# Six buffers for left forms and four for raw weights in the up projection of a hybrid block's gated MLP

## The chip, the cores and the metric

The kernel runs on one core of a Trainium2 chip as a single program. The metric is the device time of one execution in microseconds. Three runs of the kernel before gave a median of 2439.43 us (2439.18 to 2440.35).

## The reference

One decoder block on x of 1024 tokens by 1024 channels: three token mixers side by side (HGRN2, differential attention, RWKV-7), gated and projected; a cross attention to 256 memory tokens; a gated MLP with a causal convolution of width 3; a final RMSNorm. All in float32. The change lies in the MLP:

```python
def conv_gated_ffn(h, w_up, conv_w, conv_b, w_down):
    u, v = jnp.split(h @ w_up, 2, axis=-1)          # 1024 -> 2 x 2816
    u = lax.conv_general_dilated(u, conv_w[:, None, :], window_strides=(1,),
                                 padding=[(CONV_W - 1, 0)],
                                 dimension_numbers=('NWC', 'WIO', 'NWC'),
                                 feature_group_count=D_FF) + conv_b
    return (jax.nn.silu(u) * v) @ w_down            # 2816 -> 1024
```

## The kernel before, in words

Every float32 matrix product is made of three products of a shorter type: each operand is split into a high part (a cast) and a low part (the rest), and hi·hi, hi·lo and lo·hi are summed in PSUM.

**Up projection** (`ffn_up`). The 2816 channels of u and of v are worked through in 22 pairs f = 0 to 21, of 128 channels of u and 128 of v. Instead of the eight block products of a 2 x 2 by 2 x 2 block product, seven are made, of sums of blocks (the scheme of Strassen and Winograd). A pair loads two raw weight tiles of 512 KB (`load`, L1345, on the SP queue): the first holds blocks A11 and A12, the second A21 and A22. From them `left` makes up to seven **left forms** in this order: A11, S2, S3, S1, A12, A22, S4, of which S1 to S4 are sums that POOL makes (L1311). Each form becomes a tile `wf`: its high part is cast by ACT (L1318), its low part is subtracted (L1319) by DVE and POOL in turn. `prod` (L1326) multiplies a form with a right form of the activations: 12 matmuls of 128x512, named here after the right form: A11 with B11, S2 with T2, S3 with T3, S1 with T1, A12 with B21, A22 with T4, S4 with B22. So T2(f) is the product of pair f that needs S2, and B22(f), which needs S4, is the last of its pair. For the first six pairs (`ne` = 6) the products B11 and B21 are made ahead (`ahead`), between the transposes of the trunk before, and kept in DRAM; these pairs have 5 products, or 60 matmuls, left, the others 7, or 84.

DVE reads the products: u2 (L1386) after T2, u3 (L1388) after T3, the halves of vt (L1390, L1395) and of u (L1397). Then come the convolution and the gate: y by ACT (L1399), two steps on DVE (L1400, L1401), SiLU on ACT (L1402), the product with vt (L1403) and the store to DRAM (L1404).

**Buffers.** The forms have 4 buffers: the tags whi and wlo of a pool, two each, and a form uses them in turn. The raw tiles of the pairs have 6: two of the tag raw, and the tags r2 to r5 of the pool `res`, one each; the raw tiles of the six pairs ahead have four, raw twice, r4 and r5. r2 and r3 hold the trunk's normalised rows until its last transposes.

**Down projection** (`ffn_down`). The weights of each of 22 steps (wdr, 512 KB, L1445) go into r2, r3, r4, r5 in turn; wd is their cast on ACT (L1449) and their rest (L1450, POOL for even f, DVE for odd f), ap the same for the activations acr (L1447, L1452, L1453); 48 matmuls follow per step (L1439, ps_dn).

**What sets the order.** The program is written pair by pair; the compiler's scheduler then puts the instructions of each engine into an order of its own by a simulated timeline, and hands out the buffers of a tag in that order. So PE takes products of neighbouring pairs in alternation, and an instruction that waits holds up all behind it on its engine or queue.

Of the kernel before, what the change touches and what calls it, by code (L numbers as in the profile page):

```python
# [96 lines left out]
class K:  # L97
# [1197 lines left out]

    def left(self, r1, r2, which, sp):

        nc = self.nc  # L1300
        V, A, G = nc.vector, nc.scalar, nc.gpsimd
        q = {f"A{n}{k + 1}": r[:, 4 * k:4 * k + 4, :] for n, r in ((1, r1), (2, r2)) if r is not None for k in range(2)}
        sums = {"S1": ("A21", "A22", ALU.add), "S2": ("S1", "A11", ALU.subtract), "S3": ("A11", "A21", ALU.subtract),
                "S4": ("A12", "S2", ALU.subtract)}

        def get(n):
            if n not in q:
                a, b, op = sums[n]
                a, b = get(a), get(b)
                q[n] = sp.tile([P, 4, P], F32, tag=n, name=n, bufs=2 if n in ("S1", "S2") else 1)  # L1310
                G.tensor_tensor(out=q[n], in0=a, in1=b, op=op)  # L1311
            return q[n]

        for n in which:
            x = get(n)
            self.nform = getattr(self, "nform", 0) + 1
            f = self.wp.tile([P, 2, 4, P], F32R, tag=("whi", "wlo")[self.nform % 2], name="wf")
            A.copy(out=f[:, 0], in_=x)  # L1318
            (V if self.nform % 2 else G).tensor_tensor(out=f[:, 1], in0=x, in1=f[:, 0].bitcast(F32), op=ALU.subtract)  # L1319
            yield f  # L1320
# [9 lines left out]
    def ffn_up(self, X, act, part, spill):  # L1330

        nc, tc, I = self.nc, self.tc, self.I
        V, A, G, T = nc.vector, nc.scalar, nc.gpsimd, nc.tensor
        with tc.tile_pool(name="up", bufs=1) as sp:
            col = lambda j, f: self.pc("ffn_conv_w", NFF * j + f) if j < 3 else self.pc("ffn_conv_b", f)
            nraw = itertools.count()
            u = sp.tile([P, S + 2], F32, name="u")
            G.memset(u[:, 0:2], 0.0)
            ne = part.shape[1]

            def load(m, bufs=6):
                n = next(nraw) % bufs
                r = self.wp.tile([P, NK, P], F32, tag="raw", name="raw") if n < 2 else \
                    self.res.tile([P, NK, P], F32, tag=f"r{n + 6 - bufs}", name="raw")
                nc.sync.dma_start(out=r, in_=I["t_up"][m])  # L1345
                return r

            def copy(nm, src):
                s1 = sp.tile([P, 512], F32, tag="s1", name=nm, bufs=3)
                A.copy(out=s1, in_=src)  # L1350
                return s1

            def bank(f):
                return self.tps.tile([P, 512], F32, tag="t", name="ps_a") if f % 2 == 0 else \
                    self.dps.tile([P, 1024], F32, tag="d", name="ps_a")[:, 0:512]

            def ahead(f):
                forms, a = self.left(load(f, 4), None, ("A11", "A12"), sp), bank(f)
                self.prod(a, next(forms), X["B11"], True, True)
                nc.sync.dma_start(out=part[0, f], in_=copy("s1", a))  # L1360
                yield
                self.prod(a, next(forms), X["B21"], False, True)
                c = spill.tile([P, 512], F32, tag="acr", name="c11")
                A.copy(out=c, in_=a)
                nc.sync.dma_start(out=part[1, f], in_=c)
                yield

            def pair(f, rs):

                forms = self.left(*rs, ("S2", "S3", "S1", "A22", "S4") if f < ne else ("A11", "S2", "S3", "S1", "A12", "A22", "S4"), sp)  # L1370
                if f < ne:
                    s1 = sp.tile([P, 512], F32, tag="s1", name="s1", bufs=3)
                    nc.sync.dma_start(out=s1, in_=part[0, f])
                else:
                    a = self.tps.tile([P, 512], F32, tag="t", name="ps_a")
                    self.prod(a, next(forms), X["B11"], True, True)
                    s1 = copy("s1", a)
                if f < ne:
                    nc.sync.dma_start(out=u[:, 2:514], in_=part[1, f])
                vt = self.res.tile([P, S], F32, tag=f"r{6 + f % 2}", name="vt")  # L1380
                b = self.mps.tile([P, 512], F32, tag="m", name="ps_b2")
                cd = self.dps.tile([P, 1024], F32, tag="d", name="ps_cd")
                c, d = cd[:, 0:512], cd[:, 512:1024]
                u2, u3 = (sp.tile([P, 512], F32, tag=t, name=t) for t in ("u2", "u3"))
                self.prod(b, next(forms), X["T2"], True, True)
                V.tensor_tensor(out=u2, in0=b, in1=s1, op=ALU.add)  # L1386
                self.prod(c, next(forms), X["T3"], True, True)
                V.tensor_tensor(out=u3, in0=c, in1=u2, op=ALU.add)  # L1388
                self.prod(d, next(forms), X["T1"], True, True)
                V.tensor_tensor(out=vt[:, 512:1024], in0=d, in1=u3, op=ALU.add)  # L1390
                if f >= ne:
                    self.prod(a, next(forms), X["B21"], False, True)
                    A.copy(out=u[:, 2:514], in_=a)
                self.prod(c, next(forms), X["T4"], False, True)
                V.tensor_tensor(out=vt[:, 0:512], in0=c, in1=u2, op=ALU.add)  # L1395
                self.prod(d, next(forms), X["B22"], False, True)
                V.tensor_tensor(out=u[:, 514:1026], in0=d, in1=u2, op=ALU.add)  # L1397
                y = self.res.tile([P, S], F32, tag=f"r{f % 2}", name="y")
                A.activation(out=y, in_=u[:, 2:], func=AF.Identity, scale=col(2, f), bias=col(3, f))  # L1399
                V.scalar_tensor_tensor(out=y, in0=u[:, 1:S + 1], scalar=col(1, f), in1=y, op0=ALU.mult, op1=ALU.add)  # L1400
                V.scalar_tensor_tensor(out=y, in0=u[:, 0:S], scalar=col(0, f), in1=y, op0=ALU.mult, op1=ALU.add)  # L1401
                A.activation(out=y, in_=y, func=AF.Silu)  # L1402
                V.tensor_tensor(out=y, in0=y, in1=vt, op=ALU.mult)  # L1403
                (nc.gpsimd if f >= NFF - 2 else nc.sync).dma_start(out=act[f], in_=y)  # L1404

            prev = None
            for f in range(ne):
                g = ahead(f)
                next(g)
                if prev is not None:  # L1410
                    next(prev)
                prev = g
            next(prev)
            rs = [load(0), load(NFF)]
            for f in range(NFF):
                nx = [load(f + 1), load(NFF + f + 1)] if f + 1 < NFF else None
                pair(f, rs)
                rs = nx

    def ffn_down(self, act, x2_dram, out, spill):  # L1420
        nc, tc, I = self.nc, self.tc, self.I
        V, A, G, T = nc.vector, nc.scalar, nc.gpsimd, nc.tensor
        with tc.tile_pool(name="down", bufs=1) as sp:
# [3 lines left out]
            for tg in range(2):  # L1427
# [13 lines left out]

                held = []
                for f in range(NFF):
                    wr = self.res.tile([P, DM], F32, tag=f"r{2 + next(nw) % 4}", name="wdr")
                    nc.sync.dma_start(out=wr, in_=I["ffn_w_down"][0, P * f:P * f + P, :])  # L1445
                    ar = spill.tile([P, 512], F32, tag="acr", name="acr")
                    nc.sync.dma_start(out=ar, in_=act[f, :, 512 * tg:512 * tg + 512])  # L1447
                    w = self.quad("wd", shape=(P, 2, DM))
                    A.copy(out=w[:, 0], in_=wr)  # L1449
                    (V if f % 2 else G).tensor_tensor(out=w[:, 1], in0=wr, in1=w[:, 0].bitcast(F32), op=ALU.subtract)  # L1450
                    a = self.wp.tile([P, 2, 512], F32R, tag=("whi", "wlo")[f % 2], name="ap")
                    A.copy(out=a[:, 0], in_=ar)  # L1452
                    V.tensor_tensor(out=a[:, 1], in0=ar, in1=a[:, 0].bitcast(F32), op=ALU.subtract)  # L1453
                    if f == NFF // 2:
                        for j in range(4):
                            xr.append(self.res.tile([P, DM], F32, tag=f"r{(0, 1, 6, 7)[j]}", name="xr"))
                            nc.sync.dma_start(out=xr[j], in_=x2_dram[4 * tg + j])
                    if f < NFF - tail:
                        for j in range(4):
                            step(f, j, (w[:, 0], w[:, 1]), a)  # L1460
                    else:
                        held.append((f, (w[:, 0], w[:, 1]), a))
# [93 lines left out]
```

## Time and profile before

| | |
|---|---|
| median of 3 runs | 2439.43 us |
| profiled execution | 2440.76 us |
| its span | 2438.9 us (1.9 us lie around it) |
| mean granted TensorE clock | 0.989 |
| PE busy | 2338.0 us, 96% of the span |
| pairs of the up projection | about 1776 to 2199 us |
| down projection | about 2173 to 2439 us |

Times of rows are microseconds from the start of the span. Matmuls are pipelined, so that one has a duration of 0.39 us in the rows while the next starts 0.23 us later; a stall of PE is read from the idle time in square brackets. The wait views put an idle time down to the semaphore that came last.

### The profile page before, as it was taken

How to read it: one execution, taken by the hardware profiler on the slowest of the kernel's cores; microseconds unless marked ns; L12 is line 12 of the kernel's file. 1: busy time of each engine (PE TensorE's matmuls, PEld its weight loads, DVE VectorE, ACT ScalarE, POOL GpSimd, SP SyncE). 2: the span in 40 equal slices, each digit the busy share in tenths (PEclk: the TensorE clock that was granted, in tenths of full speed). 3: DMA queues.
4: the chain of work that ended last, by engine and by line, in shares of the span. 5: the costliest groups of instructions: out<-in, count | busy, mean ns of one | idle time of the engine just before them, and what ended most of it. 6: DMA issues, size and time to landing. Idle time of an engine off the chain costs nothing. (4 is left out here: it accounts for less than half of the span.)

```text
span 2438.9 us, 34709 instructions
## 1 busy us (share of the span) xinstructions
PE 2338.0 (96%) x14120; PEld 1908.3 (78%) x14120; DVE 1272.0 (52%) x1937; ACT 884.3 (36%) x1350; POOL 686.7 (28%) x558
## 2 busy tenths in 40 slices
PE   7999999999999999999999999999889999989998
PEld 7887768686778887878877778888667888878887
DVE  6446375747425557464554464544545555564422
ACT  7542213231314435344442223443333433343321
POOL 1011011010112323333231530240464555553210
PEclk9999999999999999999999999999999999999999
DMA  8654213131212111111114563233443222246541
GB/s 305 225 165 130 83 57 96 57 96 40 96 53 76 61 52 36 44 44 53 44 43 156 188 209 95 87 96 121 154 145 108 87 78 84 90 136 232 164 138 48
DMA packets 101183, 260.35 MB, mean 107 GB/s; under 512 B 26144, under 2 KB 30880, under 8 KB 101024
## 3 DMA queue, kind: packets, MB, share of 16 engines
q1 hardware_dynamic: 99584, 254.06, 31.6%
q0 software_dynamic: 1008, 3.67, 0.4%
q8 instruction: 111, 1.82, 0.3%
q14 instruction: 48, 0.39, 0.1%
q10 hardware_dynamic: 432, 0.41, 0.0%
HBM read 197.28 MB, written 60.82 MB: 106 GB/s over the span
## 5 line engine op out<-in xcount | busy, mean ns | idle before, releaser
L155 PE MATMUL ps_d<-hThi,whi 128*128 128x512 f32 x1056 | 426.0, 404 | 2.6 <-DVE Ktt L261 2.2
L157 PE MATMUL ps_d<-hTlo,whi 128*128 128x512 f32 x1056 | 424.3, 402 | 0.0
L159 PE MATMUL ps_d<-hThi,wlo 128*128 128x512 f32 x1056 | 424.1, 402 | 0.0
L140 ACT CAST whi<-raw 128x1024 fp32r<-128x1024 f32 (+1 forms) x170 | 166.9, 988 | 332.2 <-PE ps_d L157 156.6
L1439 PE MATMUL ps_dn<-wd,ap 128*128 128x512 f32 x1056 | 241.7, 391 | 7.1 <-DVE ap L1453 6.3
L1439 PEld LDWEIGHTS ps_dn<-wd,ap 128*128 128x128 f32 x1056 | 199.0, 189 | 49.3 <-DVE ap L1453 6.8
L155 PEld LDWEIGHTS ps_d<-hThi,whi 128*128 128x128 f32 x1056 | 199.9, 189 | 45.1 <-issue 3.2
L157 PEld LDWEIGHTS ps_d<-hTlo,whi 128*128 128x128 f32 x1056 | 199.9, 189 | 42.9 <-issue 4.6
L159 PEld LDWEIGHTS ps_d<-hThi,wlo 128*128 128x128 f32 x1056 | 199.7, 189 | 42.7 <-issue 4.2
L143 DVE TENSOR_TENSOR wlo<-raw,whi 128x1024 fp32r<-128x1024 f32 (+1 forms) x125 | 157.7, 1269 | 136.3 <-ACT whi L140 136.3
L143 POOL TENSOR_TENSOR wlo<-raw,whi 128x1024 fp32r<-128x1024 f32 (+1 forms) x45 | 96.2, 2139 | 435.3 <-ACT whi L140 390.0
L1318 ACT CAST wf<-S 128x512 fp32r<-128x512 f32 x88 | 54.6, 622 | 160.5 <-PE ps_cd L1326 74.3
L1453 DVE TENSOR_TENSOR ap<-acr,ap 128x512 fp32r<-128x512 f32 x44 | 37.4, 851 | 134.0 <-ACT ap L1452 127.6
L1113 POOL TENSOR_SCALAR ms<-ms 128x1 f32<-128x1 f32 x33 | 10.8, 327 | 267.1 <-ACT xn L1112 144.8
L1450 POOL TENSOR_TENSOR wd<-wdr,wd 128x1024 fp32r<-128x1024 f32 x22 | 54.5, 2479 | 107.9 <-ACT wd L1449 107.9
L1319 POOL TENSOR_TENSOR wf<-S,wf 128x512 fp32r<-128x512 f32 x44 | 62.9, 1429 | 64.0 <-ACT wf L1318 63.7
L1452 ACT CAST ap<-acr 128x512 fp32r<-128x512 f32 x44 | 27.3, 622 | 143.2 <-PE ps_dn L1439 121.9
L159 PE MATMUL ps_d<-ohi,wlo 128*128 128x512 f32 x192 | 76.2, 397 | 2.4 <-DVE wlo L143 2.4
L745 DVE CUSTOM_DVE_ANT_0 a_p<-ps_s,a_bias 128x512 f32<-128x512 f32 (+3 forms) x96 | 51.7, 552 | 50.3 <-PE ps_s L743 45.0
L755 ACT ACTIVATE a_p<-a_p,a_nm 128x128 f32<-128x128 f32 (+7 forms) x64 | 49.2, 770 | 75.5 <-POOL a_nm L751 58.0
L155 PE MATMUL ps_d<-ohi,whi 128*128 128x512 f32 x192 | 75.5, 393 | 0.7 <-ACT whi L140 0.7
L157 PE MATMUL ps_d<-olo,whi 128*128 128x512 f32 x192 | 75.5, 393 | 0.0
(423 smaller groups left out, 5276.8 us busy)
## 6 DMA issues: line engine op xcount, KB each, us to landing
raw<-t_in SPq DMA_DIRECT2D x66, 512.0 KB, 3.6
raw<-t_up SPq DMA_DIRECT2D x50, 512.0 KB, 3.5
wdr<-ffn_w_down SPq DMA_DIRECT2D x44, 512.0 KB, 4.1
th_dram<-th SPq DMA_DIRECT2D x24, 512.0 KB, 2.8
mth<-th_dram SPq DMA_DIRECT2D x24, 512.0 KB, 3.7
acr<-act_dram SPq DMA_DIRECT2D x44, 256.0 KB, 2.7
act_dram<-y SPq DMA_DIRECT2D x20, 512.0 KB, 2.6
raw<-t_kv SPq DMA_DIRECT2D x16, 512.0 KB, 4.8
```

Source lines behind the costliest of these rows:

```text
L140: nc.scalar.copy(out=hi, in_=raw)
L143: eng.tensor_tensor(out=lo, in0=raw, in1=hi.bitcast(F32), op=ALU.subtract)
L155: nc.tensor.matmul(o, lhsT=hi[:, k, :], rhs=xhi(k, h), start=(k == 0), stop=False)
L157: nc.tensor.matmul(o, lhsT=hi[:, k, :], rhs=xlo(k, h), start=False, stop=False)
L159: nc.tensor.matmul(o, lhsT=lo[:, k, :], rhs=xhi(k, h), start=False, stop=(k == nk - 1))
L745: V.tensor_tensor_reduce(out=p_[:, a:b], in0=ps[:, 0:b - a], in1=bias[:, 1024 - n + a:1024 - n + b], op0=ALU.add, op1=ALU.max, scale=1.0, ...
L755: A.activation(out=pr[c][:, 0:n], in_=pr[c][:, 0:n], func=AF.Exp, bias=nm[:, c:c + 1], accum_out=Z[:, c:c + 1])
L1318: A.copy(out=f[:, 0], in_=x)
L1319: (V if self.nform % 2 else G).tensor_tensor(out=f[:, 1], in0=x, in1=f[:, 0].bitcast(F32), op=ALU.subtract)
L1439: T.matmul(ps[j][c], lhsT=a[:, p, P * j:P * j + P], rhs=w[q][:, 512 * c:512 * c + 512], start=(f == 0 and n == 0), stop=(f == NFF - 1 and ...
L1450: (V if f % 2 else G).tensor_tensor(out=w[:, 1], in0=wr, in1=w[:, 0].bitcast(F32), op=ALU.subtract)
L1453: V.tensor_tensor(out=a[:, 1], in0=ar, in1=a[:, 0].bitcast(F32), op=ALU.subtract)
```

## The change

`left` takes the number of buffers as a parameter. The pairs pass 6: four as before, and r2 and r3 for two more forms. `load` uses four buffers only, for the pairs as for the work ahead, counted on: even pairs have r4 and r5, odd pairs the two of raw. The down projection begins its round of four with r4 instead of r2.

```diff
-    def left(self, r1, r2, which, sp):
+    def left(self, r1, r2, which, sp, slots=4):
...
             self.nform = getattr(self, "nform", 0) + 1
-            f = self.wp.tile([P, 2, 4, P], F32R, tag=("whi", "wlo")[self.nform % 2], name="wf")
+            n = self.nform % slots
+            f = self.wp.tile([P, 2, 4, P], F32R, tag=("whi", "wlo")[n % 2], name="wf") if n < 4 else \
+                self.res.tile([P, 2, 4, P], F32R, tag=f"r{n - 2}", name="wf")
...
-            def load(m, bufs=6):
-                n = next(nraw) % bufs
+            def load(m):
+                n = next(nraw) % 4
                 r = self.wp.tile([P, NK, P], F32, tag="raw", name="raw") if n < 2 else \
-                    self.res.tile([P, NK, P], F32, tag=f"r{n + 6 - bufs}", name="raw")
+                    self.res.tile([P, NK, P], F32, tag=f"r{n + 2}", name="raw")
...
-                forms, a = self.left(load(f, 4), None, ("A11", "A12"), sp), bank(f)
+                forms, a = self.left(load(f), None, ("A11", "A12"), sp), bank(f)
...
-                forms = self.left(*rs, (...), sp)
+                forms = self.left(*rs, (...), sp, 6)
...
-                    wr = self.res.tile([P, DM], F32, tag=f"r{2 + next(nw) % 4}", name="wdr")
+                    wr = self.res.tile([P, DM], F32, tag=f"r{2 + (next(nw) + 2) % 4}", name="wdr")
```

The scheduler makes a new order of it on every engine; lines after L1316 move down by two. Three places:

**SP queue, first loads of the pairs.** raw_14600 and raw_14602 are the tiles of pair 0, raw_14604 and raw_14606 of pair 1, raw_14711 and raw_14713 of pair 2, raw_14818 the first of pair 3; s1 and c11 belong to the products made ahead. Before:

```order
L1345 DMA raw_14600<-t_up 128x1024
L1345 DMA raw_14602<-t_up 128x1024
L1365 DMA part_dram_14357<-c11_14540 128x512
L1373 DMA s1_14608<-part_dram_14357 128x512
L1373 DMA s1_14715<-part_dram_14357 128x512
L1360 DMA part_dram_14357<-s1_14561 128x512
L1373 DMA s1_14822<-part_dram_14357 128x512
L1365 DMA part_dram_14357<-c11_14579 128x512
L1345 DMA raw_14818<-t_up 128x1024
L1345 DMA raw_14604<-t_up 128x1024
L1345 DMA raw_14606<-t_up 128x1024
```

After:

```order
L1347 DMA raw_14602<-t_up 128x1024
L1367 DMA part_dram_14357<-c11_14501 128x512
L1362 DMA part_dram_14357<-s1_14522 128x512
L1347 DMA raw_14604<-t_up 128x1024
L1347 DMA raw_14606<-t_up 128x1024
L1367 DMA part_dram_14357<-c11_14540 128x512
L1347 DMA raw_14711<-t_up 128x1024
L1375 DMA s1_14608<-part_dram_14357 128x512
L1375 DMA s1_14715<-part_dram_14357 128x512
```

The loads of pair 1 stand where those of pair 0 stood, ahead of the four loads of s1, and those of pair 0 still earlier (raw_14600 is three rows above the piece); pair 2 is now the one that waits for buffers of an earlier pair.

**ACT, the casts of the first pairs.** Each row L1318 (L1320 after) makes the high part of one form; the numbers are S2_14618, S1_14616, raw_14602 (A22) and S4_14686 for pair 0, S2_14725, S3_14743, S1_14723, raw_14606 (A22) and S4_14793 for pair 1, S2_14832, S3_14850 and S1_14830 for pair 2. Before:

```order
L1318 CAST wf_14670<-raw_14602 128x512
L1260 CAST B22hi_14321<-ps_T_14344 128x4x128
L1318 CAST wf_14688<-S4_14686 128x512
L1318 CAST wf_14727<-S2_14725 128x512
L1318 CAST wf_14745<-S3_14743 128x512
L1318 CAST wf_14761<-S1_14723 128x512
L1318 CAST wf_14777<-raw_14606 128x512
L1318 CAST wf_14795<-S4_14793 128x512
L1318 CAST wf_14834<-S2_14832 128x512
L1399 ACTIVATE y_14704<-u_14364,par_70 128x1024
L1318 CAST wf_14868<-S1_14830 128x512
```

After:

```order
L1320 CAST wf_14727<-S2_14725 128x512
L1260 CAST B22hi_14321<-ps_T_14337 128x4x128
L1320 CAST wf_14670<-raw_14602 128x512
L1260 CAST B22hi_14321<-ps_T_14344 128x4x128
L1320 CAST wf_14688<-S4_14686 128x512
L1320 CAST wf_14761<-S1_14723 128x512
L1320 CAST wf_14745<-S3_14743 128x512
L1320 CAST wf_14852<-S3_14850 128x512
L1320 CAST wf_14777<-raw_14606 128x512
L1320 CAST wf_14868<-S1_14830 128x512
L1320 CAST wf_14795<-S4_14793 128x512
L1320 CAST wf_14834<-S2_14832 128x512
```

The cast for T2(1) moves from behind S4 of pair 0 to ahead of its A22, and the cast of S3 of pair 2 from behind y of pair 0 to ahead of the last two forms of pair 1, while S2 of pair 2 stays the first cast behind S4 of pair 1. PE's products follow: behind T2(0) now come T2(1), T3(1) and T1(0), where T1(0) stood alone, and the products of S2 and S3 of pair f+2 now both stand directly behind B22(f).

**The end of the up projection, SP and ACT.** wdr_17462, 17496, 17530, 17564, 17598 and 17632 are the weights of steps 0 to 5 of the down projection, y_17033 and y_17171 the results of pairs 18 and 19. SP before:

```order
L1445 DMA wdr_17462<-ffn_w_down 128x1024
L1445 DMA wdr_17496<-ffn_w_down 128x1024
L1404 DMA act_dram_12077<-y_17033 128x1024
L1445 DMA wdr_17530<-ffn_w_down 128x1024
L1445 DMA wdr_17564<-ffn_w_down 128x1024
L1404 DMA act_dram_12077<-y_17171 128x1024
L1445 DMA wdr_17598<-ffn_w_down 128x1024
L1445 DMA wdr_17632<-ffn_w_down 128x1024
L1445 DMA wdr_17666<-ffn_w_down 128x1024
L1445 DMA wdr_17700<-ffn_w_down 128x1024
```

SP after:

```order
L1447 DMA wdr_17598<-ffn_w_down 128x1024
L1447 DMA wdr_17496<-ffn_w_down 128x1024
L1447 DMA wdr_17564<-ffn_w_down 128x1024
L1447 DMA wdr_17632<-ffn_w_down 128x1024
L1406 DMA act_dram_12077<-y_17171 128x1024
L1449 DMA acr_17600<-act_dram_12077 128x512
L1449 DMA acr_17634<-act_dram_12077 128x512
L1459 DMA xr_17850<-x2_dram_12076 128x1024
L1449 DMA acr_17668<-act_dram_12077 128x512
L1459 DMA xr_17846<-x2_dram_12076 128x1024
L1449 DMA acr_17702<-act_dram_12077 128x512
L1447 DMA wdr_17530<-ffn_w_down 128x1024
```

ACT after, where wf_17361 is S3 of pair 21, the form of T3(21), and wf_17427 and wf_17275 are S4 of pair 21 and A22 of pair 20:

```order
L1320 CAST wf_17427<-S4_17425 128x512
L1320 CAST wf_17343<-S2_17341 128x512
L1320 CAST wf_17275<-raw_17042 128x512
L1401 ACTIVATE y_17171<-u_14364,par_70 128x1024
L1451 CAST wd_17500<-wdr_17496 128x1024
L1404 ACTIVATE y_17171<-y_17171 128x1024
L1395 COPY u_14364<-ps_a_17182 128x512
L1320 CAST wf_17361<-S3_17359 128x512
```

The weights, which SP issued in twos between the stores of y, now go out in a block of five behind y of pair 18 (step 0 is one row above the piece), and those of step 2 (wdr_17530, in r2, which holds the form of B22(21)) only far behind it. On ACT the cast of wd_17500 (step 1) stands ahead of the cast for T3(21).

## Rows read from the trace of the kernel before

**Rows 1.** Windows: length, busy (and count) of PE, PEld, DVE, ACT, POOL; PEclk, DMA share, GB/s.

```profile
1772.00:1787.00 15.00, 10.72 (x49) 8.31 (x48) 6.54 (x9) 4.34 (x8) 9.59 (x9) 0.98 0.59 211
1787.00:1806.70 19.70, 18.05 (x72) 13.76 (x71) 9.85 (x12) 7.21 (x9) 11.96 (x10) 0.93 0.36 107
1806.70:1823.20 16.50, 14.45 (x61) 11.02 (x61) 8.90 (x10) 5.31 (x7) 11.03 (x8) 1.00 0.44 144
1823.20:1839.10 15.90, 14.44 (x60) 11.00 (x60) 9.52 (x13) 5.41 (x7) 7.58 (x6) 1.00 0.38 132
1839.10:1855.70 16.60, 14.55 (x61) 11.07 (x61) 9.17 (x10) 5.31 (x7) 11.15 (x8) 1.00 0.35 127
1855.70:1871.00 15.30, 14.59 (x62) 11.44 (x63) 8.94 (x12) 5.40 (x8) 7.21 (x6) 1.00 0.29 93
1890.00:2150.00 260.00, 259.35 (x1139) 213.22 (x1140) 146.67 (x155) 103.76 (x151) 144.48 (x102) 1.00 0.25 83
2150.00:2199.00 49.00, 41.88 (x172) 33.62 (x171) 36.64 (x28) 24.33 (x32) 26.48 (x13) 0.93 0.50 167
```

**Rows 2.** Waits of PE, 1770 to 1892: us in total, times, longest.

```profile
PE ps_b L1326 <- ACT wf L1318: 4.9, 5, 2.1
PE ps_cd L1326 <- ACT wf L1318: 3.1, 4, 0.9
PE ps_cd L1326 <- DVE u L1388: 2.2, 1, 2.2
PE ps_a L1326 <- ACT wf L1318: 1.5, 2, 0.8
PE ps_b L1326 <- POOL wf L1319: 1.3, 2, 0.6
```

**Rows 3.** Timeline of PE: start, duration, instruction, idle time before and releaser.

```profile
1781.13 0.47 PE L1326 MATMUL ps_cd<-T1hi,wf 128*128 128x512 f32 x1 [2.17 <-DVE u L1388]
1786.21 0.70 PE L1326 MATMUL ps_b<-T2hi,wf 128*128 128x512 f32 x1 [2.11 <-ACT wf L1318]
```

**Rows 4.** Timeline of DVE, ahead of T1(0).

```profile
1779.69 0.69 DVE L1319 TENSOR_TENSOR wf<-S,wf 128x512 fp32r<-128x512 f32 x1
```

**Rows 5.** Timeline of the SP queue: loads of raw tiles.

```profile
1760.96 1.82 SPq L1345 DMA_DIRECT2D raw<-t_up  x2
1773.83 1.28 SPq L1345 DMA_DIRECT2D raw<-t_up  x3
```

**Rows 6.** Timeline of POOL: sums of pair 1.

```profile
1780.51 3.77 POOL L1311 TENSOR_TENSOR S<-raw 128x512 f32<-128x512 f32 x3 [4.69 <-DMA raw<-t_up]
```

**Rows 7.** Timeline of ACT: the cast for T2(2).

```profile
1799.04 0.62 ACT L1318 CAST wf<-S 128x512 fp32r<-128x512 f32 x1 [2.04 <-PE ps_cd L1326]
```

**Rows 8.** The page, sections 5 and 6: low part of wd on POOL; loads, median us to landing.

```profile
L1450 POOL TENSOR_TENSOR wd<-wdr,wd 128x1024 fp32r<-128x1024 f32 x22 | 54.5, 2479 | 107.9 <-ACT wd L1449 107.9
raw<-t_up SPq DMA_DIRECT2D x50, 512.0 KB, 3.5
wdr<-ffn_w_down SPq DMA_DIRECT2D x44, 512.0 KB, 4.1
```

**Rows 9.** Timeline of DVE at the end of the up projection.

```profile
2177.11 3.37 DVE L1450 TENSOR_TENSOR wd<-wdr,wd 128x1024 fp32r<-128x1024 f32 x1
2180.41 2.82 DVE L1453 TENSOR_TENSOR ap<-acr,ap 128x512 fp32r<-128x512 f32 x1
```

**Rows 10.** Waits of PE, 2150 to 2200.

```profile
PE ps_dn L1439 <- DVE ap L1453: 6.3, 1, 6.3
PE ps_dn L1439 <- DVE u L1397: 0.8, 1, 0.8
```

**Rows 11.** Timeline of ACT at the end: SiLU, copy of u, cast of wd.

```profile
2177.22 1.06 ACT L1402 ACTIVATE y<-y 128x1024 f32<-128x1024 f32 x1 [1.94 <-DVE y L1401]
2178.19 0.57 ACT L1393 COPY u<-ps_a 128x512 f32<-128x512 f32 x1
2179.17 1.05 ACT L1449 CAST wd<-wdr 128x1024 fp32r<-128x1024 f32 x1
```

More of the change, by code (lines that the diff above doesn't have):

```diff
@@ L1368, in pair @@
             def pair(f, rs):
-                forms = self.left(*rs, ("S2", "S3", "S1", "A22", "S4") if f < ne else ("A11", "S2", "S3", "S1", "A12", "A22", "S4"), sp)
+                forms = self.left(*rs, ("S2", "S3", "S1", "A22", "S4") if f < ne else ("A11", "S2", "S3", "S1", "A12", "A22", "S4"), sp, 6)
                 if f < ne:
```

## The prediction

> **What bounds the kernel now.** I read the windows first [rows 1]. Between 1890 and 2150 us, which is most of the up projection, PE is busy 259.35 of 260 us: nothing is left to gain there, and each late form would be a loss. The same row gives a price for a matmul: 260 / 1139 = 0.2283 us, so a product of 12 costs 2.74 us. The windows ahead of it and the one behind it are not full. A stretch's loss is its length less its matmuls times 0.2283. For the four windows from 1806.7 to 1871 that is 16.5 - 13.9 = 2.6, 15.9 - 13.7 = 2.2, 16.6 - 13.9 = 2.7 and 15.3 - 14.2 = 1.1, together 8.6 us; for 1787 to 1806.7 it is 19.7 - 16.4 = 3.3; for 2150 to 2199 it is 49 - 39.3 = 9.7. In three of them the granted clock is below full as well (0.98, 0.93 and 0.93): between the levels 1.2 and 2.4 GHz, that is some time at the lower one behind a stall.
>
> Next the waits of PE in the first pairs [rows 2]: eleven waits for the high part of a left form, two for a low part, one for u. The timeline shows the two long ones [rows 3]: T1(0) at 1781.13 after 2.17 us, because DVE made a low part first [rows 4], and T2(1) at 1786.21 after 2.11. Why that form was late is on POOL and SP: POOL stood idle 4.69 us until 1780.51 for a raw tile and then made three sums, 3.77 us [rows 6]; the tiles of pair 0 were issued at 1760.96, those of pair 1 only from 1773.83 on [rows 5]. The remaining waits repeat in each pair and are short, 0.6 to 0.9 us. Their pattern is one cast: ACT is idle until B22(0) has ended and then casts the form for T2(2) in 0.62 us [rows 7]; with four buffers the form must wait for the buffer that the fourth form before it held.
>
> The end has one large wait, 6.3 us for DVE's ap [rows 10], with DVE slowed in front of it: 3.37 us for a low part of wd and 2.82 for one of ap [rows 9].
>
> **The change, part by part.** All is set against the profiled execution, 2440.76 us, 1.33 above the median.
>
> *(a) The first loads.* The tiles of pair 1 go out in the place of those of pair 0, at about 1761 instead of 1773.8, 13 us earlier [rows 5]. Its sums (three at 1.26 us [rows 6]) and the cast for T2(1) then end well ahead of 1779, the end of T2(0). T2(1) and T3(1) come between T3(0), T2(0) and T1(0), so DVE has 5.5 us for u in place of none. Both long waits go: 2.17 + 2.11 = 4.3 us. The low clock behind them goes too: 0.07 of 19.7 plus 0.02 of 15 us, 1.7 us [rows 1]. **Plus 6.0** (3 if the low clock and one half of a wait come back elsewhere). The tile of pair 2 that now stands ahead of the loads of s1 waits for S4 of pair 0 on POOL, which is idle there; I cost it at nothing. If it were late, u of pair 0 would be late by as much, behind the cover of 5.5 us.
>
> *(b) The short waits of pairs 1 to 6.* They lose 8.6 us, and 3.3 - 1.4 (low clock) = 1.9 in the window before: 10.5. With six buffers a form waits for the sixth one before it. Counting in the written order, T3(f+2) now takes the place of T2(f+1), long done, T1(f+2) that of T3(f+1); only T2(f+2) takes that of S4 of pair f, so it still waits for B22(f). The order shows just that: S2 of pair 2 is cast directly behind the last form of pair 1, and T2(2) is the product behind B22(0). This wait stays for four pairs, at (4.9 - 2.1) / 4 = 0.7 to 0.9 us each [rows 2], 3.2 us. **Plus 7.3**, between 3 and 10.5. The Trainium skill, page "Perfetto Trace Analysis", section "Identifying Performance Opportunities", says that one gap repeated for a stretch on the engine that should be full can mean that buffers for the next tile are missing. The rows agree on the place; by the rule taken alone the whole 10.5 would go and the sum would be 3.2 us better than mine; the row of the cast that waits for B22 [rows 7], and the order, keep me from it.
>
> *(c) The middle pairs.* Four raw buffers instead of six: the tile of pair f+2 can only be loaded once A22 of pair f has been cast and its low part made. Where the order is worst, the chain starts at the end of a B22, whose buffer this A22 takes: cast 0.62 and hand-off 0.2, low part about 1, load 3.5 [rows 8], four sums of 1.26 on POOL [rows 6], cast 0.62 and hand-off: 11 to 12.1 us. PE has 46 matmuls in that time, 10.5 us. The difference is 0.5 to 1.6 us. In the new order I find this twice in 16 pairs, since the order now repeats over several pairs and not in each; before, the stretch had nothing to lose. I take 1.2 each: **minus 2.4**, from 0 to 27 (every pair at 1.7, the rival below).
>
> *(d) The end.* Before, 9.7 us are lost. After, in the order's sequence: the cast for T3(21) stands behind that of wd of step 1, whose load starts when A22 of pair 20 is used up. Load 4.1 [rows 8], cast of wd 1.05, SiLU 1.06, copy of u 0.57 [rows 11], cast 0.62 make 7.4 us; T1(20) and T4(20) cover 5.5: 1.9 lost. The low parts of T3(21) and of its follower: 1.0, by the short waits of rows 2. The wait for u at B22(21) stays, 0.8 [rows 10]. The weights of step 2 can't be loaded before B22(21) has ended: 4.1 + 1.05 + hand-offs, 5.2, against 0.8 and the 12 matmuls of steps 0 and 1 that are left, 2.7: 1.7. Their low part, 2.48 us on POOL [rows 8], against six matmuls, 1.4: 1.1. Together 6.5. The clock took 0.07 of 49, 3.4 us; spread over several short waits I take 2. That is 8.5 against 9.7, **plus 1.2**. The bounds are wide: if the wait of 6.3 us stays beside the new ones, minus 5; if the low clock does not come at all and two of the waits are covered, plus 6.
>
> Sum: 6.0 + 7.3 - 2.4 + 1.2 = 12.1 us. 2440.76 - 12.1 = 2428.7 for the profiled execution, **2427 for the median**.
>
> **The rivals.**
>
> *Slower: the raw tiles run out in the middle.* The place is POOL's idle time for DMA in pairs 6 to 21, ahead of S1. For it speaks the length of the chain in (c), longer than its cover in its worst place, and a stretch in which PE has no slack. Against it: the load itself takes 3.5 us of a pair's 84 matmuls, 19.2 us, and most pairs in the order have more than 46 matmuls between the chain's ends. Terms (a), (b) and (d) are worth 14.5, so it decides from 14.5 / 16 = 0.9 us per pair. At the chain's worst, 1.7 us in all 16, it costs 27: 2440 - 14.5 + 27 = about 2452. With a mean of 1.1 it gives 2442.
>
> *No change: the buffers are not the ones that are short, and the end gets worse.* The two new buffers belong to fixed forms; if the order in which buffers are handed out still ties each cast to the last product of the pair before, (b) gives nothing: the change would not do what it says. With (a) at 6.0, (c) at 2.4 and the end at minus 5 that is 1.4 us slower than before by the sum, about 2441. For it speaks that ACT's casts keep following B22 in the new order; against it, that the casts of S3 do move.
>
> *A larger gain.* The rule on repeated gaps holds in full, and the end is freed, since fewer wd tiles arrive in a burst and DVE is not slowed as in rows 9: 3.2 + 4.8 more, about 2419. For it: the loads of weights spread out, one block of five and then single ones. Against: each of them lies on the way to a product.
>
> **How the numbers follow.** The forecast has 0.58, the larger gain 0.14, no change 0.15, slower 0.13. A measurement of this kernel tells about 0.2%, 4.9 us, from no change; the forecast and the larger gain lie beyond it. So faster 0.72, same 0.15, slower 0.13. The range goes from 2416 (the larger gain and a little of the bounds of (d)) to 2441 (no change taken in); the slower case is left out and some of the edges.
>
> **What would show it.** Right: no wait above 1 us between 1776 and 1800, and B22(0) ending near 1793 (five products, 13.7 us, behind 1779); the windows of pairs 1 to 6 at about 14.5 us for 60 matmuls, each with one wait of 0.7 to 0.9 behind B22; two waits of about 1 us in the middle; several of 1 to 2 us at the end and none of 6. Wrong: idle time of PE in each middle pair with POOL waiting for t_up ahead of it; a wait of more than 4 us after 2150; a cast of S3 that still waits for B22.

## The result and the profile after

The changed kernel takes 2453.86 us (median of 4 runs, 2450.2 to 2454.62) against 2439.89 us for the kernel before in the same comparison (2439.18 to 2441.78). The ratio is 1.0052 (95% interval 1.004 to 1.0064): **slower by 14 us**, where 12 us less had been forecast. The profiled execution took 2450.2 us, span 2448.4.

The windows of the changed kernel, with the columns and stretches of [rows 1]:

```profile
1772.00:1787.00 15.00, 13.86 (x61) 10.96 (x60) 8.64 (x9) 4.31 (x8) 10.49 (x8) 1.00 0.50 156
1787.00:1806.70 19.70, 16.58 (x69) 12.38 (x68) 10.12 (x12) 7.20 (x9) 12.26 (x10) 1.00 0.36 122
1806.70:1823.20 16.50, 14.22 (x60) 10.78 (x59) 8.62 (x11) 5.31 (x7) 5.86 (x5) 1.00 0.45 144
1823.20:1839.10 15.90, 13.38 (x55) 10.32 (x54) 9.65 (x9) 4.67 (x6) 9.79 (x8) 0.94 0.28 89
1839.10:1855.70 16.60, 15.05 (x62) 11.70 (x61) 9.84 (x11) 5.42 (x7) 6.87 (x5) 0.95 0.37 125
1855.70:1871.00 15.30, 14.59 (x65) 11.71 (x64) 8.77 (x9) 5.85 (x8) 10.21 (x8) 1.00 0.19 58
1890.00:2150.00 260.00, 246.56 (x1059) 200.92 (x1059) 131.87 (x142) 94.14 (x138) 140.53 (x98) 0.98 0.23 77
2150.00:2199.00 49.00, 47.71 (x208) 38.50 (x207) 30.04 (x32) 19.17 (x27) 12.54 (x9) 1.00 0.34 112
```

From 1890 to 2150, where PE had been busy 259.35 us, it is now busy 246.56, with 1059 matmuls for 1139. The first window has 61 matmuls for 49, and the last one 208 for 172: the loss is in the middle.

To compare equal work I count the matmuls between two points in the order of instructions and take 0.2268 us for each, the spacing in products without a wait (12 start 2.72 us apart). What a stretch takes beyond that is its loss. The points are the starts of T2(0), B22(0), B22(6), B22(19) and B22(21):

| us lost between | T2(0), B22(0) | B22(0), B22(6) | B22(6), B22(19) | B22(19), B22(21) |
|---|---|---|---|---|
| before | 6.4 | 13.0 | 1.0 | 9.4 |
| after | 2.5 | 15.5 | 20.0 | 2.2 |

To these come the waits behind B22(21), 0.95 us before and 3.55 after, and 0.2 us less between the first product made ahead and T2(0). Together: 4.1 less in the head, 2.5 more in pairs 1 to 6, 19.0 more in the middle, 4.6 less at the end, 12.8 us more. The spans differ by 9.5 only, as the first product made ahead began 3.3 us earlier in this execution; the instructions ahead of it stand in the same order on PE, DVE, ACT and POOL in all fourteen kernels, and in the profiles it begins anywhere from 1706 to 1720 us. So stages are compared here, and times by medians.

The waits of PE from 1770 to 1892 us, as in [rows 2] (us in total, times, longest):

```profile
PE ps_cd L1328 <- DVE vt L1392: 4.5, 4, 1.8
PE ps_b L1328 <- ACT wf L1320: 3.7, 5, 0.8
PE ps_cd L1328 <- DVE vt L1397: 3.1, 4, 0.8
PE ps_a L1328 <- ACT wf L1320: 0.7, 1, 0.7
```

The casts cost 4.4 us instead of 9.5, and the wait for u is gone, but two new waits, for vt, take 7.6. Here is how they come about in pair 1, on PE and on DVE:

```profile
1801.87 0.50 PE L1328 MATMUL ps_cd<-T4hi,wf 128*128 128x512 f32 x1 [0.79 <-DVE vt L1392]
...
1805.71 0.50 PE L1328 MATMUL ps_cd<-B22hi,wf 128*128 128x512 f32 x1 [0.78 <-DVE vt L1397]
...
1809.45 0.50 PE L1328 MATMUL ps_b<-T2hi,wf 128*128 128x512 f32 x1 [0.71 <-ACT wf L1320]
```

```profile
1801.12 0.69 DVE L1392 TENSOR_TENSOR vt<-ps_cd,u 128x512 f32<-128x512 f32 x1
1804.96 0.69 DVE L1397 TENSOR_TENSOR vt<-ps_cd,u 128x512 f32<-128x512 f32 x1 [3.15 <-PE ps_cd L1328]
```

T1, T4 and B22 of a pair now stand one behind the other, here as in pairs 0 to 3. T3 and T4 sum up in one half of the tile ps_cd, T1 and B22 in the other. T4 starts only when DVE has read T1's half (1801.12 + 0.69 = 1801.81), B22 only when it has read T4's (1805.65): two stalls of 0.8 us in a pair, then that for T2's cast, 0.71. Neither reading touches the half that is written next; the program's wait is for the tile. Before, matmuls of the next pair stood in each of these places and covered them: ahead of T4(1) the first two of T3(2), which themselves waited 0.87 us for a cast, and ahead of B22(1) the other ten.

A stall costs more than its brackets say: T4(1) starts 3.67 us behind T1(1), 0.95 more than a product's 2.72, where the brackets have 0.79. And behind T4(3), which waits 1.8 us, the granted clock falls to 0.94 and 0.95 in the windows from 1823.2 to 1855.7.

The middle, 1892 to 2180 us:

```profile
PE ps_cd L1328 <- DVE vt L1392: 7.0, 3, 3.1
PE ps_a L1328 <- POOL wf L1321: 5.7, 2, 2.9
PE ps_cd L1328 <- ACT wf L1320: 1.4, 2, 0.7
PE ps_b L1328 <- DVE wf L1321: 0.2, 1, 0.2
```

Four stalls of about 3 us, 11.9 together, make more than half of the 20.0, one of each of two kinds in every six pairs: B11 waits for a low part on POOL (at 1950 and 2074), T4 for vt on DVE (at 1995 and 2118). The clock takes about another 5: it is 0.98 over the 260 us, with 0.83 from 1950 to 1960 and 0.70 from 2118 to 2128, behind two of these stalls. The second kind at T4(11), on PE, DVE and POOL:

```profile
1995.53 0.47 PE L1328 MATMUL ps_cd<-T4hi,wf 128*128 128x512 f32 x1 [3.08 <-DVE vt L1392]
```

```profile
1986.76 0.69 DVE L1390 TENSOR_TENSOR u<-ps_cd,u 128x512 f32<-128x512 f32 x1
1987.37 1.27 DVE L1402 SCALAR_TENSOR_TENSOR y<-u,par,y 128x1024 f32<-128x1024 f32 x1
1988.68 2.19 DVE L1403 SCALAR_TENSOR_TENSOR y<-u,par,y 128x1024 f32<-128x1024 f32 x1
1990.79 1.78 DVE L1321 TENSOR_TENSOR wf<-S,wf 128x512 fp32r<-128x512 f32 x1
1992.50 2.28 DVE L1405 TENSOR_TENSOR y<-y,vt 128x1024 f32<-128x1024 f32 x1
1994.70 0.68 DVE L1392 TENSOR_TENSOR vt<-ps_cd,u 128x512 f32<-128x512 f32 x1
```

```profile
1989.74 6.17 POOL L1311 TENSOR_TENSOR S<-raw 128x512 f32<-128x512 f32 x3
```

T1(11) is done by 1992.45 (1995.53 - 3.08), but its reading, L1392, stands on DVE behind three operations that take 2.19, 1.78 and 2.28 us. Elsewhere the same ones take 1.28, 0.69 and 1.23. POOL makes three sums in that time, at 2.06 us each instead of 1.26 [rows 6].

POOL also waits for raw tiles now, 27.8 us between 1892 and 2150, where it had no such wait before:

```profile
POOL S L1311 <- DMA raw<-t_up: 27.8, 9, 7.4
```

At the end (2180 to 2220) there is no wait above 1.2 us, where ap had cost 6.3 [rows 10]:

```profile
PE ps_dn L1441 <- POOL wd L1452: 1.2, 1, 1.2
PE ps_dn L1441 <- ACT wd L1451: 0.8, 1, 0.8
PE ps_dn L1441 <- DVE u L1399: 0.8, 1, 0.8
PE ps_cd L1328 <- POOL wf L1321: 0.4, 1, 0.4
```

### The profile page after: what moved, and what is told of

Same layout as the page of the kernel before. It is cut to its first block, busy times and chain, and to the rows that moved or that the text cites. A ratio compares the mean times of both kernels' runs of the same rounds, so it can differ in the third digit from the quotient of the medians.

```text
span 2448.4 us, 34652 instructions
## 1 busy us (share of the span) xinstructions
PE 2342.6 (96%) x14120; PEld 1911.9 (78%) x14120; DVE 1276.5 (52%) x1937; ACT 886.0 (36%) x1350; POOL 684.5 (28%) x558
## 3 DMA queue, kind: packets, MB, share of 16 engines
q0 software_dynamic: 1008, 3.67, 0.4%
## 5 line engine op out<-in xcount | busy, mean ns | idle before, releaser
L1320 ACT CAST wf<-S 128x512 fp32r<-128x512 f32 x88 | 54.6, 622 | 124.6 <-PE ps_cd L1328 88.0
L1311 POOL TENSOR_TENSOR S<-raw 128x512 f32<-128x512 f32 x44 | 64.3, 1473 | 64.3 <-DMA raw<-t_up 45.3
L1320 ACT CAST wf<-raw 128x512 fp32r<-128x512 f32 x66 | 41.0, 623 | 104.0 <-PE ps_cd L1328 63.2
```

## The experiments

Two theories for the time lost. **O**: six form buffers let the scheduler draw the products of one pair together, and that order costs. **R**: four raw tiles are too few. Losses per stage of all twelve runs stand in the table at the end of this section; it ends at B22(21). Times are medians, ratios are to the kernel before in the same comparison.

**1. Four forms, four raw tiles.** Against the changed kernel:

```diff
-                forms = self.left(*rs, (...), sp, 6)
+                forms = self.left(*rs, (...), sp, 4)
```

> Changed kernel with four form buffers again (four raw tiles, down projection from r4, as changed). Theory O, the six form buffers make the scheduler put the products of one pair next to each other, and that costs the time in pairs 1 to 19: here the order of products is that of before, so the middle (pairs 7 to 19) loses about 1 us and not 19, pairs 1 to 6 lose 13 as before; with the head's 7 us gained, 2428 to 2433. Theory R, four raw tiles are too few: the middle still loses about 19, 2444 to 2448.

2439.32 us, ratio 1.0009 (0.9996 to 1.0023): between the two. The middle loses 7.3 us, 6.3 more than before, in small waits (1885 to 2180):

```profile
PE ps_dn L1441 <- DVE ap L1455: 6.3, 1, 6.3
PE ps_cd L1328 <- DVE vt L1392: 2.2, 4, 0.6
PE ps_a L1328 <- ACT wf L1320: 1.8, 7, 0.3
```

The order of products is that of before but for small pieces. So R is true for a third of the middle's loss, 6.3 of 19.0, and the gain of the end is not there: the wait for ap is back.

**2. Six forms, six raw tiles.** Two tiles of their own for the forms; load and down projection as before; s1 and spill shortened to make room:

```diff
-                self.res.tile([P, 2, 4, P], F32R, tag=f"r{n - 2}", name="wf")
+                sp.tile([P, 2, 4, P], F32R, tag=f"f{n}", name="wf")
```

> Six form buffers (two of them tiles of their own) with the six raw tiles and the order of loads and of the down projection of before; to make room s1 has two buffers instead of three and acr/c11 three instead of four. Theory O: T1, T4 and B22 of a pair stand next to each other, waits of T4 for vt of 0.8 us in each of pairs 1 to 4, and 10 to 20 us lost in the middle: 2448 to 2458. Theory R: six raw tiles suffice, the middle loses 1 to 2 us, 2433 to 2442.

2462.05 us, ratio 1.0096 (1.0081 to 1.0111), slower still, and 4 us above what theory O gave. The middle loses 15.3 us, in the same kinds of stall, half as deep (1885 to 2180):

```profile
PE ps_a L1328 <- POOL wf L1321: 5.0, 3, 1.7
PE ps_cd L1328 <- DVE vt L1392: 3.0, 2, 1.5
PE ps_cd L1328 <- ACT wf L1320: 1.4, 2, 0.7
PE ps_b L1328 <- ACT wf L1320: 1.4, 2, 0.7
```

With 6.3 for four raw tiles alone and 14.3 for six forms alone the parts add up to 20.6; both together lost 19.0 more. O is the larger part. The shortened buffers may have their share in this kernel's 23 us, so only its middle is used. There s1 is in use too; no copy into it waits in the middle for DVE to give a buffer back, but that its shorter buffer has no part in the order is not shown.

**3. The raw tiles counted on.** Against the kernel before:

```diff
-                n = next(nraw) % bufs
+                n = (next(nraw) + (4 if bufs == 6 else 0)) % bufs
```

> Kernel before, the pairs' six raw tiles counted on from where the work ahead stopped: pair 0 in r4 and r5, pair 1 in raw, pair 2 in r2 and r3. If the head's gain of 7.3 us in the changed kernel is the earlier load of pair 1: T2(1) follows T2(0) without a wait, 2432 to 2434. If it is the form buffers: 2439 to 2441.

2428.67 us, ratio 0.9959 (0.9942 to 0.9975). The head loses 1.0 us instead of 6.4, so its gain is the early load of pair 1 and needs no form buffer. (In the table, "on" stands for raw tiles counted on.) Not expected: the end loses 2.2 instead of 9.4. Of these 7.2 us 1.2 come back behind B22(21), where PE waits 1.6 us for a cast of ap.

**4. The same, and the down projection from r4.**

```diff
-                    wr = self.res.tile([P, DM], F32, tag=f"r{2 + next(nw) % 4}", name="wdr")
+                    wr = self.res.tile([P, DM], F32, tag=f"r{2 + (next(nw) + 2) % 4}", name="wdr")
```

> As the kernel with the raw tiles counted on, and the down projection begins with r4. If the gain at the end in the changed kernel (5 us net) comes from the later and differently ordered loads of the weights: 4 to 7 us below the former, 2426 to 2429. If it comes from the order of the products: within 2 us of it.

2427.84 us, ratio 0.9954 (0.9937 to 0.997): no difference to run 3.

**5. Six forms and four raw tiles in pairs 0 to 5 only**, from pair 6 on as in run 3:

```diff
+                n = next(nraw)
+                n = n % 4 if bufs == 4 else (n + 4) % 6
...
+                forms = self.left(*rs, (...), sp, 6 if f < ne else 4)
```

> Six form buffers and four raw tiles in pairs 0 to 5 only; from pair 6 on four form buffers and six raw tiles, counted on as in the kernel with the raw tiles counted on (2428.7). The order of products from pair 7 on is that of before. If the order made by six form buffers is what costs: the middle loses 1 us again, pairs 0 to 6 lose 18 as in the changed kernel instead of 14.6, so 2430 to 2434. If the six form buffers pay in the first pairs: 2422 to 2427.

2435.38 us, ratio 0.9991 (0.9979 to 1.0003). The middle loses 1.0 us, as expected; pairs 0 to 6 lose 22.4, more than expected, with the waits for vt (1755 to 1895):

```profile
PE ps_cd L1328 <- DVE vt L1393: 6.1, 6, 1.8
PE ps_b L1328 <- ACT wf L1320: 3.7, 5, 0.8
PE ps_cd L1328 <- DVE vt L1398: 3.1, 4, 0.8
```

**6. The same with a PSUM tile of its own for T1 and B22 in pairs 0 to 5:**

```diff
-                c, d = cd[:, 0:512], cd[:, 512:1024]
+                c, d = cd[:, 0:512], cd[:, 512:1024] if f >= ne else self.tps.tile([P, 512], F32, tag="t", name="ps_d2")
```

> As the former, and in pairs 0 to 5 the products of T1 and B22 have a PSUM tile of their own, so that T4 needs no longer wait for the reading of T1's product, nor B22 for that of T4's. If the new waits of T4 and B22 for vt in pairs 0 to 4 come from the shared tile: they go, pairs 0 to 6 lose 6 to 10 us instead of 18, 8 to 12 us below the former, 2419 to 2424. If DVE is late there anyway: waits for vt or u stay, less than 4 us below.

2413.92 us, ratio 0.9913 (0.9894 to 0.9933), 21 us below run 5: twice what was expected. Pairs 0 to 6 lose 1.7 us. The waits for the casts are gone as well. The order of products is new once more. T3/T4 and T1/B22 have two buffers each, as they had as halves of the two tiles ps_cd; what ends is that they share a tile.

**7. That tile with four forms**, on run 3:

> Four form buffers everywhere, raw tiles counted on, and the PSUM tile of its own in pairs 0 to 5. The waits for ACT's casts of T2 and T3 (0.7 to 0.9 us each) come from the four form buffers: they stay, pairs 0 to 6 lose 12 to 15 us as without the tile, 2426 to 2430. If the shared PSUM tile holds the order back also with four buffers: 2420 to 2425.

2413.87 us, ratio 0.9909 (0.9892 to 0.9925), below the second case too. The first case is refuted: with four form buffers the casts are in time as well. One wait is left in 1755 to 1880:

```profile
PE ps_b L1326 <- DVE wf L1319: 0.3, 1, 0.3
```

Here B22(0) stands directly behind T4(0), and T4(2) directly behind T1(2), the neighbours that stalled in the changed kernel. On PE and on DVE:

```profile
1788.61 0.39 PE L1326 MATMUL ps_d<-B22hi,wf 128*128 128x512 f32 x1
...
1807.65 0.39 PE L1326 MATMUL ps_cd<-T4hi,wf 128*128 128x512 f32 x1
```

```profile
1788.81 0.69 DVE L1395 TENSOR_TENSOR vt<-ps_cd,u 128x512 f32<-128x512 f32 x1 [0.64 <-PE ps_cd L1326]
...
1810.25 0.68 DVE L1390 TENSOR_TENSOR vt<-ps_d,u 128x512 f32<-128x512 f32 x1
```

B22(0) starts before DVE reads T4(0), T4(2) 2.6 us before DVE reads T1(2). So the two stalls of a pair came from the shared tile.

**8. That tile in the changed kernel:**

> The changed kernel (six form buffers, four raw tiles, all pairs) with the PSUM tile of its own for T1 and B22 in pairs 0 to 5. If the shared tile is what undid the gain in the first pairs: they lose 2 us instead of 18, the middle still about 19: 2434 to 2441. If four raw tiles or the forms hold them: above 2445.

2434.34 us, ratio 0.9985 (0.9972 to 0.9998). In its windows the first pairs are full and the middle is much as it was:

```profile
1780.00:1890.00 110.00, 109.86 (x485) 90.68 (x484) 75.26 (x76) 42.27 (x58) 76.82 (x51) 1.00 0.37 124
1890.00:2150.00 260.00, 246.74 (x1049) 201.01 (x1048) 133.44 (x143) 95.34 (x140) 134.07 (x92) 0.97 0.23 77
```

**9. And from pair 6 on B11/B21 share a tile with T3/T4, T1/B22 have their own:**

```diff
-                    a = self.tps.tile([P, 512], F32, tag="t", name="ps_a")
+                    cd = self.dps.tile([P, 1024], F32, tag="d", name="ps_ac")
+                    a = cd[:, 512:1024]
...
-                cd = self.dps.tile([P, 1024], F32, tag="d", name="ps_cd")
-                c, d = cd[:, 0:512], cd[:, 512:1024]
+                if f < ne:
+                    cd = self.dps.tile([P, 1024], F32, tag="d", name="ps_cd")
+                c, d = cd[:, 0:512], self.tps.tile([P, 512], F32, tag="t", name="ps_d2")
```

> As the former, and from pair 6 on the shared tile holds the products B11/B21 and T3/T4 (the one read by ACT, the other by DVE), while T1/B22 has its own. If the waits of T4 for vt in the middle (3.1 us twice, with the low clock behind them about 10 of the 19 us) come from the shared tile: they go, 2424 to 2432. If DVE and POOL are too late there for any order: as the former within 4 us.

2408.76 us, ratio **0.9869** (0.9854 to 0.9883), better than expected: PE is not idle at all from 1780 to 2200.

```profile
1780.00:1890.00 110.00, 110.00 (x487) 91.09 (x486) 77.85 (x81) 43.31 (x59) 77.17 (x51) 1.00 0.38 130
1890.00:2150.00 260.00, 260.00 (x1149) 215.29 (x1148) 150.24 (x157) 101.91 (x150) 147.40 (x98) 1.00 0.25 85
2150.00:2200.00 50.00, 50.00 (x223) 41.39 (x222) 31.17 (x25) 22.47 (x28) 16.83 (x10) 1.00 0.70 241
```

With six forms and four raw tiles in all pairs the stalls for vt are gone, and those for POOL's low parts too, which I had left to the four raw tiles. As the order of products is new again, the run shows that the tile suffices to remove them, not that each was a wait for it. The raw tiles still come late: POOL waits longer for them than in the changed kernel, and PE loses nothing by it (1892 to 2150):

```profile
POOL S L1311 <- DMA raw<-t_up: 51.5, 14, 7.7
```

**10. Only the down projection from r4**, on the kernel before (the diff of run 4):

> Kernel before, only the down projection begins with r4. If the end's wait of 6.3 us for ap comes from weights of the down projection that land early and load DVE and POOL before the last pair is done: those of steps 0 and 1 now wait for pair 20's raw tiles, the wait shrinks, 2431 to 2436. If it comes from the order of the last products: 2437 to 2441, as before.

2439.14 us, ratio 1.0002 (0.9991 to 1.0012), and the end loses 9.6: the order of r2 to r5 does nothing there.

**11. The tiles of run 9 in the kernel before**, with four forms and six raw tiles:

> Kernel before with the PSUM tiles dealt out as in the fastest run (T1/B22 alone, B11/B21 with T3/T4), but four form buffers and six raw tiles as before. If the shared tile was all that cost and the buffers change nothing: 2407 to 2411, as with six and four. If six form buffers pay once the tile is out of the way: slower by what the short waits for casts and the late tiles of pair 1 take, 2414 to 2424.

2420.41 us, ratio 0.993 (0.9906 to 0.9955), in the range of the second case, but run 12 shows that it is not for want of form buffers. Of the waits for casts one is left, at T3(1); a large wait stands at the end, ahead of B21(21) at 2163 (1755 to 2220):

```profile
PE ps_ac L1326 <- DVE u L1390: 7.6, 1, 7.6
PE ps_cd L1326 <- ACT wf L1318: 1.3, 1, 1.3
```

That is a shared tile again: B21(21) waits for the reading of T3(21), which is in the other half of its tile ps_ac, and DVE comes to it late, behind four low parts of 2.32, 2.85, 3.36 and 1.75 us. On PE and on DVE:

```profile
2163.27 0.76 PE L1326 MATMUL ps_ac<-B21hi,wf 128*128 128x512 f32 x1 [7.64 <-DVE u L1390]
```

```profile
2162.45 0.68 DVE L1390 TENSOR_TENSOR u<-ps_ac,u 128x512 f32<-128x512 f32 x1
```

**12. The tiles of run 9 on run 3:**

> The same, with the six raw tiles counted on, so that pair 1's land early. If only the late tiles of pair 1 are left as a loss in the former: as fast as the fastest, 2407 to 2411. If four form buffers still cost casts: 2412 to 2420.

2406.53 us, ratio **0.9876** (0.9858 to 0.9894), as fast as run 9 within their intervals. Once the PSUM tiles are dealt out otherwise, six forms with four raw tiles and four with six make no difference that shows. What is left is how the raw tiles are counted, 14 us between runs 11 and 12. Of these the table has only 1.9 in the head, where pair 1 comes late, and 7.8 at the end, where run 12 has 1.1 us of the wait for u instead of 7.6. So dealing the tiles out otherwise does not end the tie between two halves of a tile; in runs 9 and 12 the order hides all or most of it.

| run | forms, raw tiles | T1/B22 alone | to B22(0) | to B22(6) | to B22(19) | to B22(21) | median us |
|---|---|---|---|---|---|---|---|
| 1 | 4, 4 | no | 1.0 | 15.8 | 7.3 | 8.8 | 2439.3 |
| 2 | 6, 6 | no | 4.5 | 17.4 | 15.3 | 7.5 | 2462.1 |
| 3 | 4, 6 on | no | 1.0 | 13.5 | 1.2 | 2.2 | 2428.7 |
| 4 | 4, 6 on; r4 | no | 1.0 | 14.0 | 1.1 | 2.2 | 2427.8 |
| 5 | 6, 4, then 4, 6 | no | 2.9 | 19.5 | 1.0 | 3.7 | 2435.4 |
| 6 | 6, 4, then 4, 6 | pairs 0 to 5 | 0 | 1.7 | 1.1 | 2.3 | 2413.9 |
| 7 | 4, 6 on | pairs 0 to 5 | 0 | 0.5 | 1.1 | 2.2 | 2413.9 |
| 8 | 6, 4 | pairs 0 to 5 | 0 | 0 | 22.8 | 2.4 | 2434.3 |
| 9 | 6, 4 | all | 0 | 0 | 0 | 0 | 2408.8 |
| 10 | 4, 6; r4 | no | 6.3 | 13.1 | 1.1 | 9.6 | 2439.1 |
| 11 | 4, 6 | all | 1.9 | 0 | 0 | 9.2 | 2420.4 |
| 12 | 4, 6 on | all | 0 | 0.4 | 0 | 1.4 | 2406.5 |

## Why the prediction was wrong

The forecast was 12.1 us faster; the stages of the two profiles add up to 12.8 slower. Of these 24.9 us (a) makes 1.9, (b) 9.8 and (c) 16.6, while (d) came out 3.4 better than forecast. So (b) and (c) failed.

**(a) The first loads: right, at 4.1 us for 6.0.** Both long waits went, and run 3 shows that the early load is what does it (5.4 us there). In the changed kernel about 2 us come back, as T4(0) and B22(0) wait for vt.

**(b) The short waits: the step that failed first.** "T3(f+2) now takes the place of T2(f+1), long done" was right, and so was the wait that stays for T2(f+2). But the step counted only what the forms wait for. The order that it quoted itself, T2(1), T3(1), then T1(0), takes away the products between T1, T4 and B22 of a pair, and T4 and B22 must each wait for DVE's reading of the one before, since the sums lie in two halves of one tile: 7.6 us of waits that the step did not have, 5.7 of them behind the start of B22(0). Plus 7.3 became minus 2.5. What [rows 7] show, a cast that waits for B22, was put down to the number of form buffers. Runs 6 and 7 show otherwise: with six or with four forms the casts are in time as soon as T1 and B22 have a tile of their own, in the order of products that the scheduler then makes. The rule of the Trainium skill that the prediction weighed (page "Perfetto Trace Analysis", section "Identifying Performance Opportunities") names PSUM beside SBUF as what can be short. The runs agree as to the place: the short waits of these pairs, 7.4 us for casts before without that at T2(1), shrink to 1.4 us for a low part in run 6 and 0.3 in run 7. But no sum has more buffers there than before; they only lie in other tiles.

**(c) The middle: minus 2.4 forecast, minus 19.0 measured.** The chain that the step priced, from a B22 through the load to T2, delayed no T2 there. What the runs show in its place: six forms alone lose 14.3 us (run 2), four raw tiles alone 6.3 (run 1), and the stalls lie at T4 behind DVE and at B11 behind POOL. With T1 and B22 in a tile of their own in all pairs the stretch loses nothing (run 9). The rival "slower" gave 2452 and the run 2453.9, but that is luck: POOL does wait for raw tiles where the rival said, 27.8 us, yet in run 9 it waits 51.5 and PE is never idle. Even in run 1 the loss is in waits of T4 for vt and of B11 for casts. Rows that the prediction had would have led there: DVE's operations slowed to 3.37 and 2.82 us [rows 9] were used for the end only.

**(d) The end: plus 1.2 forecast, plus 4.6 measured.** Of the waits that it listed those for u and for the high and low part of step 2 came, at 0.8, 0.8 and 1.2 us (a step has 24 matmuls in each of its two rounds, where the section on the kernel before says 48); that for the cast of T3(21) did not, nor the low clock (1.00 from 2150 to 2199). That the wait of 6.3 us goes was right. Why it goes is not settled: it is there in the kernel before and in runs 1 and 10, gone in run 3, and beginning the down projection with r4 does nothing. In run 3 two waits for casts of ap stand in its place, 1.2 and 1.6 us. Whether the raw tiles' places at the end free fewer of r2 to r5 early, or only the order of the last products differs, was not tried.

The rival "no change" had the cause in its name, that the buffers are not the ones that are short, but not the tile, and a price of 1 us. The chance of slower was put at 0.13: the prediction priced what the new buffers free and not what the new order binds.

## What to carry to other kernels

Before a stall is put down to a lack of buffers, ask what else ties the waiting instruction: here two sums in two halves of one PSUM tile made a product wait for the reading of its neighbour. Dealing the tiles out otherwise took 16 us off the kernel before (run 11) and 45 off the changed one (run 9), where more buffers had cost 14. Where a scheduler makes the order, more freedom in one resource can bring instructions together that wait for each other through another one; so read the new order pair by pair for what must be read or written between two neighbours. When both signs are possible, lay out the change's parts as a square of four kernels: the two parts here lost 6 and 14 us in the middle, and only that told which.

## What the hardware showed that I had not expected

DVE and POOL slow each other more than the prediction allowed for: at 1990 us a low part took 1.78 us and the gate's product 2.28 on DVE, against 0.69 and 1.23 elsewhere, and POOL's sums 2.06 against 1.26, while DVE's reading of PSUM, vt at 1994.70, took 0.68 as ever beside a sum on POOL. None of DVE's readings of PSUM in the pairs of the changed kernel takes more than 0.7 us. The Trainium skill, page "SBUF — State Buffer", section "SBUF: two separate sides", says that a DVE operation with two SBUF inputs and a GpSimd operation that reads SBUF share a port pair that one of them holds for a whole instruction; these rows agree: all that are slowed have two SBUF inputs, and vt, with one, is not. PE can run this stage with no idle time at all: in run 9 it is busy 420 of 420 us.
